# Norm sums taken on VectorE, and the query projection folded into 512-column matmuls

## The chip, the cores and the metric

The kernel runs on one core of a Trainium2 chip. The core has five engines that each work through a queue of their own in order: TensorE (PE, matmuls; its weight loads are listed as PEld), VectorE (DVE), ScalarE (ACT), GpSimd (POOL) and SyncE (SP, which here only issues transfers). The metric is device microseconds of one execution; the time of a kernel is the median of its runs. A profile is one more execution with the hardware profiler on.

## The reference

Two decoder layers on 256 tokens of 2048 features, batch 1, all in float32. Layer 0 mixes a causal gMLP (8 heads) with an HGRN2 recurrence (8 heads of 128 features); layer 1 mixes by forgetting attention (16 heads). Each mixer is followed by a gated MLP with a width-3 causal convolution. Cut to what the change touches:

```python
def rms_norm(x, gain):
    y = x * lax.rsqrt(jnp.mean(x * x, axis=-1, keepdims=True) + RMS_EPS)
    return y * gain

def mixer_ab(h, w_in, ...):          # layer 0, h = rms_norm(x)
    u, v, q, f, i, g = jnp.split(h @ w_in, cuts, axis=-1)
    ...
    y_b = hgrn2(q, f, i, g, lower_bound, o_gain)
    return jnp.concatenate([y_a, y_b], axis=-1) @ w_out

for l in range(2):
    h = rms_norm(x, mix_norm[l]);  x = x + mixer(h)
    h = rms_norm(x, ffn_norm[l]);  x = x + conv_ffn(h)
```

So there are four norms over the 2048 features of each token, and one projection of 2048 x 1024 for the queries `q` of the recurrence.

## The kernel before

**Tiles.** Activations lie feature-major: a tile has 128 features in its partitions and 256 tokens as columns. Every float32 operand of a large product is split into a high part and a low part (fp32r), and a product is high times high, high times low, and low times high, summed in PSUM. An activation tile `a` has 512 columns: the 256 high ones, then the 256 low ones. A weight tile `w` arrives by a transfer on SP's queue; ScalarE copies its high part `wh` (L185), VectorE subtracts for its low part `wl` (L186). This goes on for all 820 weight pieces, and TensorE consumes them in order.

**Norms.** The gain is multiplied into the activations when they are split, and the factor `Rt`, one number per token, is applied later, when a product leaves PSUM. `Norm.feed_square` adds the squares of the 16 feature tiles into `acc` (128 x 256). `Norm.finish_tok` (L466) has TensorE sum `acc` over its partitions: two small matmuls, `acc` as the stationary operand and a two-column piece of ones as the moving one (L470), which the profile counts as four. `rsq` (L425 to L430, with Ln and Exp on ScalarE between) makes `Rt` of the sums. It runs four times: at the start of layer 0, before each gated MLP, and before layer 1.

**Queries.** In `mixer_ab` the queries are projected head by head (L876), `project` with the weights stationary: per 128 features, the high weights times the 256 high columns, the high weights times the 256 low columns, and the low weights times the 256 high columns, all into the same 256 columns of a PSUM bank (L316). ScalarE then copies the even and the odd tokens into the head's tile `kq` (L877, L878), the odd ones in reverse. `project` also makes the last four blocks of the last product of the kernel; the change leaves these as they are.

**Around them.** A recurrence head is a generator `hgrn(h)` whose steps are laid between the weight pieces of the projections that come next: per head a copy to `kd` on ScalarE (L741), two products on GpSimd (L742 on `kd`, L744 on `kq`), a chain of six products on GpSimd (L750, `tot`), small diagonal matmuls on TensorE (L755), and products and copies on VectorE and ScalarE (L762 to L805). Between the heads 3 and 4, and 6 and 7, `values(j)` projects the recurrence's values (`project_tok`): there TensorE reads a mirrored copy `ar` of the activations, which GpSimd makes piece by piece (L332), in a rotation of three buffers.

**The order.** The program is written as one stream; a scheduling layer then sets each engine's queue, under the explicit "not before" ties (`held`, `tied`, `in_order`). An engine never runs past a waiting instruction.

Of the kernel before, what the change touches and what calls it, by code (L numbers as in the profile page):

```python
# [8 lines left out]
F32 = mybir.dt.float32  # L9
F32R = mybir.dt.float32r  # L10
U16 = mybir.dt.uint16
AF = mybir.ActivationFunctionType
ALU = mybir.AluOpType
AX = mybir.AxisListType

P = 128
S = 256
D = 2048
# [6 lines left out]
BLK = 32  # L25
# [9 lines left out]
LANE = 64  # L35
# [20 lines left out]
def tile_trunk(ctx: ExitStack, tc: tile.TileContext, x, pp_d, cst_d, mlev_d, msk_d,  # L56
               w_v, w_f, w_g, w_i, w_q, w_u, w_abo, w_cf, w_cqkv, w_cg, w_co, w_up, w_dn, spw_d, spb_d, out):
    nc = tc.nc
    V, SC, PE = nc.vector, nc.scalar, nc.tensor

    cp = ctx.enter_context(tc.tile_pool(name="cp", bufs=1))
    wp = ctx.enter_context(tc.tile_pool(name="wp", bufs=4))
    apool = ctx.enter_context(tc.tile_pool(name="ap", bufs=KT))
    tp = ctx.enter_context(tc.tile_pool(name="tp", bufs=2))
# [4 lines left out]
    def nm(base):  # L69
        count[0] += 1  # L70
        return f"{base}_{count[0]}"
# [3 lines left out]
    for c0, n in ((0, 1), (1, 1), (2, 2), (4, 2), (6, 2), (8, 4), (12, 4)):  # L75
        t = cp.tile([P, n, S], F32, tag=f"x{c0}", name=f"x{c0}")
# [4 lines left out]
    ones = cp.tile([P, P], F32, tag="ones", name="ones")  # L81
# [5 lines left out]
    order = mybir.DependencyInfo(mybir.DependencyClass.NoSync, mybir.DependencyReason.DATA)  # L87
    epoch = {"set": None, "load": None, "ops": []}

    def act(out_, in_, func, **kw):  # L90
        name = TABLE.get(func)
        if name is not None and name != epoch["set"]:
            ld = SC.preload_act_table_set(name)
            for o in epoch["ops"]:
                tc.add_manual_dep(ld.ins, o.ins.name, order, reason="table order")
            epoch.update(set=name, load=ld, ops=[ld])
        r = SC.activation(out_, in_, func, **kw)
        if name is not None:
            tc.add_manual_dep(r.ins, epoch["load"].ins.name, order, reason="table order")
            epoch["ops"].append(r)  # L100
        return r

    def view(ap, off, *dims):
        return bass.AP(ap.tensor, ap.offset + off, [list(ap.ap[0])] + [list(d) for d in dims])

    def back(ap):
        return view(ap, P - 1, (-1, P))
# [5 lines left out]
    def bank():  # L113
        return psum["pool"].tile([P, 512], F32, tag="px", name=nm("px"), bufs=psum["banks"])
# [11 lines left out]
    def tick():  # L126
        steps[0] += 1
        while queue and len(flight) < depth[0]:
            flight.append(queue.pop(0))
        for g in list(flight):  # L130
            if next(g, flight) is flight:
                flight.remove(g)
# [16 lines left out]
    deep = {"pool": None, "turn": 0, "dma": None}  # L149
# [39 lines left out]
    before = {}  # L189
# [6 lines left out]
    def weights(src, n, rows=None, parts=halves):  # L196
        w, wh, wl = three(n)
        in_order("w", nc.sync.dma_start(w if rows is None else w.rearrange("p (m c) -> p m c", m=rows), src))
        parts(w, wh, wl)
        for what in ("wh", "wl"):  # L200
            in_order(what, deep[what])
        return wh, wl
# [89 lines left out]
    def by_tokens(t, o):  # L292
        return view(t, o, (1, P), (P, 2))

    def to_tokens(ps):
        return view(ps, 0, (2, P), (1, 2))

    def of_tokens(ps, T):
        return view(ps, T, (2, P))

    def project(wsrc, acts, chunks=(8, 8), k0=0, run=2, parts=None):

        ps = pm.tile([P, 512], F32, tag="pm", name=nm("pm"))
        nk = sum(chunks)
        done = 0
        for c in chunks:
            lo = (k0 + done) * P
            if parts is None:
                tick()
            wh, wl = parts or weights(wsrc[:, lo:lo + c * P], c * P)  # L310
            for k1 in range(0, c, run):
                ks = range(k1, min(k1 + run, c))
                for t, os in ((wh, (0, S)), (wl, (0,))):
                    for k in ks:
                        for o in os:
                            deep["last"] = PE.matmul(to_tokens(ps), t[:, k * P:(k + 1) * P],  # L316
                                                     by_tokens(acts[done + k], o),
                                                     start=done + k + o == 0 and t is wh,
                                                     stop=t is wl and done + k == nk - 1)
            done += c  # L320
        return ps
# [82 lines left out]
    def held(r, last="wh"):  # L404

        tc.add_manual_dep(r.ins, deep[last].ins.name, order, reason="not before")
# [13 lines left out]
    def rsq(dst, src, n):  # L420
        tag = "sq" if dst.shape[-1] == S else "rm"
        cols = dst.shape[-1] if dst.shape[-1] == S else LANE // math.prod(dst.shape[1:-1])
        m, t = (tp.tile(list(dst.shape[:-1]) + [max(cols, dst.shape[-1])], F32, tag=tag, name=nm(n_))
                [..., 0:dst.shape[-1]] for n_ in ("rm", "rt"))
        V.tensor_scalar(m, src, 1.0 / n, EPS, ALU.mult, ALU.add)  # L425
        act(dst, m, AF.Ln)
        act(dst, dst, AF.Exp, scale=-0.5)
        V.scalar_tensor_tensor(t, dst, -0.5, dst, ALU.mult, ALU.mult)
        V.tensor_tensor(t, t, m, ALU.mult)
        V.scalar_tensor_tensor(dst, t, 1.5, dst, ALU.add, ALU.mult)  # L430
# [5 lines left out]
    class Norm:  # L436
# [27 lines left out]
            self.feed_square(k)  # L464

        def finish_tok(self):  # L466
            p2 = bank()
            for T in range(2):
                lhs = self.acc[:, T * P:(T + 1) * P] if not self.turn else view(self.acc, T, (2, P))
                r = PE.matmul(p2[:, 2 * T:2 * T + 2], lhs, ones[:, 0:2], start=True, stop=True)  # L470
                if "mm" in deep:
                    tc.add_manual_dep(r.ins, deep["mm"].ins.name, order, reason="not before")
            Rt = cp.tile([P, LANE], F32, tag="Rt", name=nm("Rt"), bufs=2)[:, 0:2]
            yield
            yield
            rsq(Rt, p2[:, 0:4].rearrange("p (t two) -> p t two", two=2)[:, :, 0], D)
            self.Rt = Rt

    def add_four(q, ps, z, tmp, dst, nxt, halves=1, queues=(nc.sync, nc.gpsimd)):
# [25 lines left out]
    def mixer_ab(norm):  # L505
        es = ExitStack()
        hp = es.enter_context(tc.tile_pool(name="hp", bufs=1))
# [23 lines left out]
        for g, ps in enumerate(project_first(w_v, norm, lambda: queue.append(finish()))):  # L531
# [5 lines left out]
            else:  # L537
                last = ps
        A = norm.a
# [19 lines left out]
        two = hp.tile([P, 2, P], F32, tag="pairs", name="pairs")  # L559
# [109 lines left out]
        lf, kq = [], []  # L669
# [20 lines left out]
        for j in range(2):  # L690
            ps = project_four(w_f[4 * j:4 * j + 4], A, KT)
            Rt = norm.Rt
            z, tmp = (hp.tile([P, 1024], F32, tag="E", name=nm(n), bufs=2) for n in ("zf", "tmp"))
            for T in range(2):
                SC.activation(cols4(z[:, T * 512:(T + 1) * 512]), of_rows(ps[T]), AF.Copy, scale=Rt[:, T:T + 1])
            t = hp.tile([P, 1024], F32, tag="o", name=nm("turn"), bufs=2)
# [137 lines left out]
        def values(j):  # L834
            ps = project_tok(w_i[j], norm, lambda: hp.tile([P, 512], F32R, tag="ar", name=nm("ar"), bufs=3))
            itok = hp.tile([P, 2, 512], F32, tag="tok", name=nm("itok"), bufs=2)
            for T in range(2):
                SC.activation(cols2(itok[:, T]), of_two(ps[T]), AF.Copy, scale=Rr[:, T:T + 1])
            itoks.append((itok, steps[0]))
# [29 lines left out]
        for h in range(NH):  # L869
            if h in (4, 7):  # L870
                values(len(itoks))
            while len(kq) <= h:
                tick()
            if h % 4 == 0:
                os_.append(hp.tile([P, 2, 512], F32, tag="o", name=nm("o"), bufs=2))
            ps = project(w_q[h], A)  # L876
            SC.activation(kq[h][:, 2], of_tokens(ps, 0), AF.Copy)  # L877
            SC.activation(back(kq[h][:, 1]), of_tokens(ps, 1), AF.Copy)  # L878
            queue.append(hgrn(h))
        for j in range(2):  # L880
            ps = project_four(w_g[4 * j:4 * j + 4], A, KT)
# [16 lines left out]
        for j in range(2):  # L898
            ps = project_four(w_u[4 * j:4 * j + 4], A, KT)
            z, tmp = (hp.tile([P, 1024], F32, tag="E", name=nm(n), bufs=2) for n in ("zu", "tmp"))  # L900
            for T in range(2):
                SC.activation(cols4(z[:, T * 512:(T + 1) * 512]), of_rows(ps[T]), AF.Copy, scale=Rt[:, T:T + 1])
            t = hp.tile([P, 1024], F32, tag="tok", name=nm("turn"), bufs=2)
# [12 lines left out]
        def stretch(q, ks, **kw):  # L916
            return project_four(w_abo[4 * q:4 * q + 4], product, KT, ks=ks, **kw)

        ahead = None
        for q in range(4):  # L920
            if q == 0:

                ps = stretch(0, (0, 2, 4, 6, 8, 10), more=True)
                ahead = stretch(1, (0, 2, 4, 6), more=True)
                stretch(0, (12, 14), ps=ps)
            elif q == 1:
                ps = stretch(1, (8, 10, 12, 14), ps=ahead)
            else:
                ps = stretch(q, range(0, KT, 2))
            z = hp.tile([P, 2, 512], F32, tag="tok", name=nm("zo"), bufs=2)  # L930
# [323 lines left out]
    def ffn(l, norm, last):  # L1254
# [142 lines left out]
        return nxt  # L1397

    norm = mixer_ab(Norm(C_MIX))
    norm = ffn(0, norm, False)  # L1400
    norm = mixer_c(norm)
# [81 lines left out]
```

## Time and profile before

| what | us |
|---|---|
| median of 3 runs | 2170.12 (2169.95 to 2170.48) |
| the profiled execution | 2170.68 |
| its span on the core | 2168.9 |
| TensorE matmuls busy | 2162.4 |
| VectorE busy | 1599.7 |
| ScalarE busy | 1310.1 |
| GpSimd busy | 470.7 |

The granted TensorE clock is 1.00 over the span. Times in the profile's views count from the span's start. A matmul's duration in a view holds its way through the pipeline; the pace at which matmuls follow each other is read from their starts. "Idle before" is the time in which an engine stood still ahead of an instruction, with what ended it.

### The profile page before, as it was taken

The numbers are of one execution on the slowest core, as the hardware profiler recorded it, in microseconds if no ns is written. First come the engines' busy times: TensorE is split into PE (matmuls) and PEld (weight loads), VectorE is DVE, ScalarE is ACT, GpSimd is POOL, SyncE is SP. The second block draws the span as 40 slices with busy tenths as digits, with TensorE's granted clock in tenths as the row PEclk, the third lists the DMA queues.
The fourth block names the chain that finished last, engine by engine and source line by source line (L and its number), as shares of the span: only waits on it lengthen the run. The fifth ranks groups of instructions, "written<-read, shape, count | busy, mean of one in ns | idle before, by whom it ended". The sixth has DMA issues, their size and how long they took to land.

```text
span 2168.9 us, 32423 instructions
## 1 busy us (share of the span) xinstructions
PE 2162.4 (100%) x10874; PEld 1900.3 (88%) x10874; DVE 1599.7 (74%) x2265; ACT 1310.1 (60%) x1903; POOL 470.7 (22%) x867
## 2 busy tenths in 40 slices
PE   9999999999999999999999999999999999999999
PEld 8998888888888888888888888888888888888888
DVE  7888768777577657776887787877786577667766
ACT  6677766666466545654565556766666466456642
POOL 0352231212012002111133443221211012012102
PEclk9999999999999999999999999999999999999999
DMA  8755777777667767776777767777777677666866
GB/s 304 220 172 175 219 223 236 235 229 238 217 214 223 223 213 212 230 235 205 248 230 223 243 203 215 225 240 223 234 238 223 201 236 220 227 213 208 247 214 187
DMA packets 492680, 483.61 MB, mean 223 GB/s; under 512 B 115168, under 2 KB 460400, under 8 KB 492384
## 3 DMA queue, kind: packets, MB, share of 16 engines
q1 hardware_dynamic: 465888, 453.27, 66.4%
q0 software_dynamic: 24896, 26.05, 5.2%
q10 hardware_dynamic: 1728, 2.21, 0.4%
q8 instruction: 85, 1.39, 0.3%
q14 instruction: 83, 0.68, 0.1%
HBM read 435.24 MB, written 2.11 MB: 202 GB/s over the span
## 4 chain that ended last, share of the span: by engine, by line
PE 94%; DVE 2%; DMA 2%; SPq 1%; ACT 1%; issue 0%; DVEq 0%; ACTq 0%; POOLq 0%
PE pm L360 25%; PE pm L361 25%; PE pm L362 25%; PE pm L341 4%; PE pm L343 4%; PE pm L342 4%; PE pm L316 2%; PE pm L236 1%; DVE wl L186 1%; SPq L380 1%; DMA w<-in_w_up 1%; DMA zt<-tmp 1%; PE pm L260 0%; DVE tmp L373 0%; ACT wh L185 0%
## 5 line engine op out<-in xcount | busy, mean ns | idle before, releaser
L186 DVE TENSOR_TENSOR wl<-w,wh 128x1024 fp32r<-128x1024 f32 (+1 forms) x820 | 991.6, 1217 | 460.6 <-ACT wh L185 451.1
L185 ACT ACTIVATE wh<-w 128x1024 fp32r<-128x1024 f32 (+1 forms) x820 | 856.7, 1049 | 624.4 <-PE pm L362 459.3
L360 PE MATMUL pm<-wh,a 128*128 128x512 f32 x1728 | 655.8, 379 | 0.0
L361 PE MATMUL pm<-wl,a 128*128 128x512 f32 x1728 | 655.2, 379 | 0.2
L362 PE MATMUL pm<-wh,a 128*128 128x512 f32 x1728 | 654.9, 379 | 0.0
L380 POOL DMA_DIRECT2D zt<-tmp x413 | 223.5, 549 | 1134.8 <-DVE tmp L373 1022.9
L361 PEld LDWEIGHTS pm<-wl,a 128*128 128x128 f32 x1728 | 326.6, 189 | 47.1 <-DVE wl L186 1.0
L362 PEld LDWEIGHTS pm<-wh,a 128*128 128x128 f32 x1728 | 326.6, 189 | 46.3
L360 PEld LDWEIGHTS pm<-wh,a 128*128 128x128 f32 x1728 | 326.6, 189 | 46.3
L360 PE MATMUL pm<-wh,hid 128*128 128x512 f32 x688 | 260.8, 379 | 0.0
L361 PE MATMUL pm<-wl,hid 128*128 128x512 f32 x688 | 260.8, 379 | 0.0
L362 PE MATMUL pm<-wh,hid 128*128 128x512 f32 x688 | 260.8, 379 | 0.0
L341 PE MATMUL pm<-wh,a 128*128 128x512 f32 x416 | 158.7, 381 | 0.4 <-ACT a L398 0.4
L343 PE MATMUL pm<-wh,a 128*128 128x512 f32 x416 | 157.8, 379 | 0.0
L342 PE MATMUL pm<-wl,a 128*128 128x512 f32 x416 | 157.7, 379 | 0.0
L360 PEld LDWEIGHTS pm<-wh,hid 128*128 128x128 f32 x688 | 130.0, 189 | 18.5
L362 PEld LDWEIGHTS pm<-wh,hid 128*128 128x128 f32 x688 | 130.0, 189 | 18.4
L361 PEld LDWEIGHTS pm<-wl,hid 128*128 128x128 f32 x688 | 130.0, 189 | 18.4
L1289 ACT ACTIVATE conv<-zt,pp 128x256 f32<-128x256 f32 x176 | 95.8, 589 | 71.5 <-DMA zt<-tmp 48.4
L380 POOL DMA_DIRECT2D turn<-tmp x160 | 86.9, 551 | 211.4 <-DVE tmp L373 179.3
L1290 DVE SCALAR_TENSOR_TENSOR conv<-zt,pp,conv 128x255 f32<-128x255 f32 x176 | 80.2, 480 | 54.4 <-ACT conv L1289 42.7
L373 DVE STREAM_TRANSPOSE tmp<-z 128x512 f32<-128x512 f32 x120 | 98.1, 850 | 7.1 <-ACT z L1275 5.1
(255 smaller groups left out, 2207.7 us busy)
## 6 DMA issues: line engine op xcount, KB each, us to landing
w<-in_w_up SPq DMA_DIRECT2D x352, 512.0 KB, 5.0
w<-in_w_dn SPq DMA_DIRECT2D x176, 512.0 KB, 5.0
w<-in_w_cqkv SPq DMA_DIRECT2D x96, 512.0 KB, 4.9
w<-in_w_abo SPq DMA_DIRECT2D x32, 512.0 KB, 5.0
w<-in_w_cg SPq DMA_DIRECT2D x32, 512.0 KB, 5.2
w<-in_w_co SPq DMA_DIRECT2D x32, 512.0 KB, 4.8
zt<-tmp SPq DMA_DIRECT2D x414, 32.0 KB, 2.7
zt<-tmp POOLq DMA_DIRECT2D x413, 32.0 KB, 2.4
```

Source lines behind the costliest of these rows:

```text
L185: r = deep["wh"] = SC.activation(wh, w, AF.Copy)
L186: deep["wl"] = V.tensor_tensor(wl, w, wh.bitcast(F32), ALU.subtract)
L341: PE.matmul(to_two(ps[T]), ah, h, start=k + i == 0, stop=False)
L342: PE.matmul(to_two(ps[T]), ah, l, start=False, stop=False)
L343: deep["last"] = PE.matmul(to_two(ps[T]), al, h, start=False, stop=k + i == KT - 1)
L360: PE.matmul(to_rows(ps[T]), ah, h, start=not begun and k + i == ks[0], stop=False)
L361: PE.matmul(to_rows(ps[T]), ah, l, start=False, stop=False)
L362: deep["mm"] = deep["last"] = PE.matmul(to_rows(ps[T]), al, h, start=False, stop=not more and k + i == ks[-1] + 1)
L373: V.transpose(tmp.rearrange("p (b m i t) -> p b m i t", b=4, m=4, t=2)[:, :, :, :, T], src(T).rearrange("p (m b j) -> p b m j", m=4, b=4))
L380: queues[(a + b) % len(queues)].dma_start(dst[BLK * b:BLK * (b + 1), :, a * n:(a + 1) * n], tmp[BLK * a:BLK * (a + 1), b * 4 * n:(b + 1) * ...
L1289: held(SC.activation(c, z, AF.Identity, bias=pp[:, cb:cb + 1], scale=w(2)))
L1290: V.scalar_tensor_tensor(c[:, 1:], z[:, :S - 1], w(1), c[:, 1:], ALU.mult, ALU.add)
```

## The change

Two edits. First, `finish_tok` no longer uses TensorE: VectorE transposes `acc` in blocks of 32 x 32, sums each block's columns, brings the four partition quarters side by side with four small copies, sums these, and copies the result out to the four quarters; `rsq` then reads that instead of PSUM. Second, the query projection gets `fold=True`: the high weights meet the high and the low columns of the activations in one 512-column matmul, high result in columns 0 to 255 and low result in 256 to 511; the low weights still go in a 256-column matmul onto the first half. One ScalarE copy takes all 512 columns to SBUF (a tile `z` in the same three-buffer rotation as `ar`), and GpSimd adds the halves, once for the even and once for the odd tokens.

```diff
     def project(wsrc, acts, chunks=(8, 8), k0=0, run=2, parts=None, fold=False):
...
+                if fold:
+                    for k in ks:
+                        PE.matmul(ps, wh[:, k * P:(k + 1) * P], view(acts[done + k], 0, (S, 2), (1, P), (P, 2)),
+                                  start=done + k == 0, stop=False, skip_group_check=True)
+                    for k in ks:
+                        deep["last"] = PE.matmul(to_tokens(ps), wl[:, k * P:(k + 1) * P],
+                                                 by_tokens(acts[done + k], 0),
+                                                 start=False, stop=done + k == nk - 1, skip_group_check=True)
+                    continue
...
         def finish_tok(self):
-            p2 = bank()
-            for T in range(2):
-                lhs = self.acc[:, T * P:(T + 1) * P] if not self.turn else view(self.acc, T, (2, P))
-                r = PE.matmul(p2[:, 2 * T:2 * T + 2], lhs, ones[:, 0:2], start=True, stop=True)
-                if "mm" in deep:
-                    tc.add_manual_dep(r.ins, deep["mm"].ins.name, order, reason="not before")
-            Rt = cp.tile([P, LANE], F32, tag="Rt", name=nm("Rt"), bufs=2)[:, 0:2]
+            t = cp.tile([P, LANE], F32, tag="Rt", name=nm("Rt"), bufs=2)
+            Rt, ssq, r, u, s = (t[:, i:i + n] for i, n in ((0, 2), (2, 2), (8, 8), (16, 32), (48, 8)))
+            sq = tp.tile([P, S], F32, tag="sq", name=nm("sq"))
+            by_block = view(self.acc, 0, (1, 2), (2 * BLK, 4), (2, BLK)) if self.turn else \
+                self.acc.rearrange("p (t g i) -> p t g i", t=2, i=BLK)
+            held(V.transpose(sq.rearrange("p (t g i) -> p t g i", t=2, i=BLK), by_block), "wl")
+            held(V.tensor_reduce(r, sq.rearrange("p (c i) -> p c i", i=BLK), AX.X, ALU.add), "wl")
             yield
+            for a in range(4):
+                held(V.tensor_copy(u[0:BLK, 8 * a:8 * a + 8], r[BLK * a:BLK * (a + 1)]), "wl")
+            V.tensor_reduce(s[0:BLK], u[0:BLK].rearrange("p (a c) -> p c a", a=4), AX.X, ALU.add)
+            for g in range(4):
+                V.tensor_copy(ssq[BLK * g:BLK * (g + 1)], view(s[0:BLK], g, (4, 2)))
             yield
-            rsq(Rt, p2[:, 0:4].rearrange("p (t two) -> p t two", two=2)[:, :, 0], D)
+            rsq(Rt, ssq, D)
...
-            ps = project(w_q[h], A)
-            SC.activation(kq[h][:, 2], of_tokens(ps, 0), AF.Copy)
-            SC.activation(back(kq[h][:, 1]), of_tokens(ps, 1), AF.Copy)
+            ps = project(w_q[h], A, fold=True)
+            z = hp.tile([P, 512], F32, tag="ar", name=nm("z"), bufs=3)
+            SC.activation(z, ps, AF.Copy)
+            for i, q in enumerate((kq[h][:, 2], back(kq[h][:, 1]))):
+                nc.gpsimd.tensor_tensor(q, view(z, i, (2, P)), view(z, S + i, (2, P)), ALU.add)
```

TensorE's queue keeps its order, without the four pairs of small matmuls. Three places of other queues move.

GpSimd, around the start of `values(1)`, after head 6's projection; `ar_1965`, `ar_2003`, `ar_2071` are the first three mirrored pieces of `values(1)`, and `kd_1584` and `kq_1007` belong to head 3. Before:

```order
L742 TENSOR_TENSOR kd_1584<-kd_1584,kq_1007 128x2x64
L744 TENSOR_TENSOR kq_1007<-kq_1007,lf_1006 128x2x64
L332 COPY ar_1965<-a_113 128x256
L332 COPY ar_1965<-a_120 128x256
L332 COPY ar_2003<-a_162 128x256
L332 COPY ar_2003<-a_169 128x256
L332 COPY ar_2071<-a_207 128x256
L332 COPY ar_2071<-a_210 128x256
L750 TENSOR_TENSOR tot_1790<-lf_1223 128x128
```

The same three mirrored pieces now (`ar_1876`, `ar_1914`, `ar_1982`); `kd_1896` and `kq_1224` are head 5's, and L894 is the pair of adds of head 6:

```order
L756 TENSOR_TENSOR kd_1896<-kd_1896,kq_1224 128x2x64
L758 TENSOR_TENSOR kq_1224<-kq_1224,lf_1223 128x2x64
L341 COPY ar_1876<-a_113 128x256
L341 COPY ar_1876<-a_120 128x256
L341 COPY ar_1914<-a_162 128x256
L894 TENSOR_TENSOR kq_1276<-z_1853 128x128 x2
L341 COPY ar_1914<-a_169 128x256
L341 COPY ar_1982<-a_207 128x256
L341 COPY ar_1982<-a_210 128x256
```

The pieces stood behind head 3's products, far ahead of their use; now they stand behind head 5's, and head 6's adds stand among them. At `values(0)` they move in the same way, from ahead of head 0's products to behind head 1's.

VectorE, at the first norm; `acc_90` is its sum of squares, `wl_...` are weight pieces of the projection that runs then, `rm_596` and `rm_605` are the first step of `rsq`. Before:

```order
L186 TENSOR_TENSOR wl_535<-w_533,wh_534 128x1024
L564 CAST msk<-kst 128x896
L659 TENSOR_TENSOR gm<-gm 128x8
L660 TENSOR_TENSOR gm<-gm 128x8
L186 TENSOR_TENSOR wl_561<-w_559,wh_560 128x1024
L569 TENSOR_TENSOR wt_511<-wt_511,cst 128x1024
L661 RECIPROCAL gm<-gm 128x8
L662 TENSOR_TENSOR gm<-gm 128x8
L663 TENSOR_TENSOR gm<-gm 128x8
L186 TENSOR_TENSOR wl_580<-w_578,wh_579 128x1024
L664 TENSOR_SCALAR gm<-gm 128x8
L425 TENSOR_SCALAR rm_596<-px_551 128x2
```

Now:

```order
L186 TENSOR_TENSOR wl_535<-w_533,wh_534 128x1024
L481 STREAM_TRANSPOSE sq_552<-acc_90 128x256
L578 CAST msk<-kst 128x896
L482 TENSOR_REDUCE Rt_551<-sq_552 128x8
L186 TENSOR_TENSOR wl_561<-w_559,wh_560 128x1024
L485 COPY Rt_551<-Rt_551 32x8 x4
L583 TENSOR_TENSOR wt_511<-wt_511,cst 128x1024
L486 TENSOR_REDUCE Rt_551<-Rt_551 32x8
L186 TENSOR_TENSOR wl_589<-w_587,wh_588 128x1024
L488 COPY Rt_551<-Rt_551 32x2 x4
L673 TENSOR_TENSOR gm<-gm 128x8
L434 TENSOR_SCALAR rm_605<-Rt_551 128x2
```

Eleven new instructions stand between the weight pieces, and `rm` stays behind the same third piece. At the other three norms the eleven stand together after one piece or around one, and `rm` comes up to two pieces earlier than before.

ScalarE, after head 7's projection; `z_2266` is the new copy, `kd` the copy of L741 (now L755), `wh_2479` and `wh_2376` the same weight piece. Before:

```order
L93 ACT_TABLE_LOAD
L877 ACTIVATE kq_1361<-pm_2283 128x128
L878 ACTIVATE kq_1361<-pm_2283 128x128
L769 ACTIVATE E_2253<-kq_1323 128x256
L741 ACTIVATE kd_2431<-kq_1361 128x2x64
L794 ACTIVATE s_366_2401<-px_2375 128x128
L796 ACTIVATE st_953<-px_2375 64x64 x2
L185 ACTIVATE wh_2479<-w_2478 128x1024
```

Now:

```order
L93 ACT_TABLE_LOAD
L892 ACTIVATE z_2266<-pm_2194 128x512
L783 ACTIVATE E_2164<-kq_1276 128x256
L808 ACTIVATE s_374_2298<-px_2272 128x128
L810 ACTIVATE st_962<-px_2272 64x64 x2
L755 ACTIVATE kd_2328<-kq_1314 128x2x64
L185 ACTIVATE wh_2376<-w_2375 128x1024
```

The copy to `kd` has moved behind three others, directly ahead of the weight piece. It reads the head's tile `kq`, which GpSimd's adds now write: where it waited for ScalarE's own copies, it now waits for GpSimd.

More of the change, by code (lines that the diff above doesn't have):

```diff
@@ L299, in of_tokens, with project @@
         return view(ps, T, (2, P))
-    def project(wsrc, acts, chunks=(8, 8), k0=0, run=2, parts=None):
+    def project(wsrc, acts, chunks=(8, 8), k0=0, run=2, parts=None, fold=False):
         ps = pm.tile([P, 512], F32, tag="pm", name=nm("pm"))
```

## The prediction

> **What bounds the kernel now.** I read the page's first part (busy time, share of the span and instructions of each engine), and then its fourth, the chain of work that ended last.
>
> ```profile
> PE 2162.4 (100%) x10874; PEld 1900.3 (88%) x10874; DVE 1599.7 (74%) x2265; ACT 1310.1 (60%) x1903; POOL 470.7 (22%) x867
> PE 94%; DVE 2%; DMA 2%; SPq 1%; ACT 1%; issue 0%; DVEq 0%; ACTq 0%; POOLq 0%
> ```
>
> TensorE is busy for 2162.4 of 2168.9 us and makes 94% of the chain. So work taken off TensorE shortens the span one for one, as long as TensorE then waits for nothing new; time on other engines counts only where TensorE comes to wait for it. Two questions follow: what TensorE's queue loses, and where its next operand now comes too late.
>
> **What leaves TensorE: the norms.** TensorE's timeline at the first and at the last of the four norms (start, duration, instruction):
>
> ```profile
> 49.51 0.38 PE L362 MATMUL pm<-wh,a 128*128 128x512 f32 x1
> 49.72 0.50 PE L470 MATMUL px<-ones,acc 128*128 128x2 f32 x4
> 50.09 0.46 PE L360 MATMUL pm<-wh,a 128*128 128x512 f32 x1
> 50.39 0.38 PE L361 MATMUL pm<-wl,a 128*128 128x512 f32 x1
> ...
> 1505.27 0.38 PE L362 MATMUL pm<-wh,a 128*128 128x512 f32 x1
> ...
> 1506.16 0.38 PE L361 MATMUL pm<-wl,a 128*128 128x512 f32 x1
> ```
>
> From L362's start to that of the second matmul behind it (L361) are 0.88 and 0.89 us. Two 512-column steps take 2 x 0.216 (next fence), so one norm costs 0.45 us of TensorE, and four cost **1.8 us**.
>
> **The queries.** Two pieces of the chain, and the group of high-weight matmuls of L316:
>
> ```profile
> 16.22 31.08 PE pm L236 x144
> 181.21 5.36 PE pm L316 x48
> L316 PE MATMUL pm<-a,wh 128*128 128x256 f32 x256 | 39.7, 278 | 0.0
> ```
>
> 144 matmuls of 512 columns take 31.08 us, 215.8 ns each; 48 of 256 columns take 5.36 us, 111.7 ns each. Two small ones cost 223.4, so each pair that becomes one saves 7.5 ns. The 256 matmuls of the group are 128 pairs: **1.0 us**. The low-weight matmuls stay. The Trainium skill ("TensorE: Matmul & The Clock Gate", Part 1, "Wait — 56ns, not 53.3ns?") gives a warm step as columns over 2.4 GHz and about 2.5 ns more; this agrees with the 215.8, but makes 109.2 ns of the 256 columns, where the trace has 111.7. By the page the 128 pairs would save 0.3 us; the measured rows decide.
>
> Together TensorE's queue gets 2.8 us shorter. All else of this part is what comes back as waits.
>
> **Norms on VectorE.** Groups of VectorE that are most like the new instructions (busy us, mean ns):
>
> ```profile
> L373 DVE STREAM_TRANSPOSE tmp<-z 128x512 f32<-128x512 f32 x120 | 98.1, 850 | 7.1 <-ACT z L1275 5.1 <-ACT z L481 1.5
> L1082 DVE TENSOR_REDUCE mxs<-sc 128x1 f32<-128x256 f32 x16 | 6.5, 409 | 0.0
> L643 DVE COPY small<-rab 32x1 f32<-32x1 f32 x4 | 0.6, 145 | 0.1
> ```
>
> The transpose has half the columns of L373's (0.43), the big reduction is like L1082 (0.41), eight copies at L643's 0.145 make 1.16, the small reduction I put at 0.2, since it has an eighth of that one's columns but can't be shorter than a small copy: some 2.2 us of VectorE per norm. The timeline of ScalarE, VectorE and TensorE behind the first norm, and one row of VectorE at the second:
>
> ```profile
> 54.64 1.05 ACT L185 ACTIVATE wh<-w 128x1024 fp32r<-128x1024 f32 x1
> 55.72 1.22 DVE L186 TENSOR_TENSOR wl<-w,wh 128x1024 fp32r<-128x1024 f32 x1 [0.49 <-ACT wh L185]
> 58.16 0.38 PE L361 MATMUL pm<-wl,a 128*128 128x512 f32 x1
> ...
> 383.40 2.36 DVE L186 TENSOR_TENSOR wl<-w,wh 128x1024 fp32r<-128x1024 f32 x2 [1.36 <-ACT wh L185]
> ```
>
> In the last three norms VectorE stands idle 1.36 us ahead of each weight piece, so two pieces take it in; I cost them at 0 (bounds 0 and 0.3). Their `Rt` then comes a piece or two earlier, and with it SP issues one transfer of `turn` two weight pieces sooner; I cost that at 0 too, since weights there are split a whole piece ahead (the second wl of the row at 383.40 belongs to the piece after next).
>
> The first norm has less room: VectorE's queue is full there, and behind `rsq` stands ScalarE's table load, then `gv`, then wh at 54.64 and its wl, which ends at 56.94, 1.22 us ahead of its matmul at 58.16. Part of the eleven fits where VectorE waited for other things; I take wh to come 0.85 later, still hidden, and charge 0.1 us. If all 2.2 us arrived there, it would be 1.0.
>
> **The adds on GpSimd.** A ScalarE copy with the new one's form, and the products on GpSimd that are most like the adds (minimum, median, maximum in ns):
>
> ```profile
> L838 ACT ACTIVATE itok<-pm,small 128x512 f32<-128x512 f32 x4 | 2.6, 681 | 0.1
> L742 POOL TENSOR_TENSOR kd<-kd,kq x8: 517/902/1486, 97.1 to 190.4; 128x128 f32<-128x128 f32 x8
> L744 POOL TENSOR_TENSOR kq<-kq,lf x8: 507/576/851, 98.1 to 191.2; 128x128 f32<-128x128 f32 x8
> ```
>
> ScalarE gives up two copies of 0.26 (L877 in the next fence, and its sister) and gets one of 0.68. A pair of adds is bounded by the fastest and the slowest product: 1.0 and 3.0 us. I take twice L744's median, **1.15 us**, since its operands, as the adds', are float32 128 x 128 read with a stride; twice L742's median would be 1.8. None of it is on TensorE, so it counts where TensorE soon needs what stands behind the adds. There are four such places; rows of `values(0)`, head 4 and `values(1)`:
>
> ```profile
> 116.28 0.26 ACT L877 ACTIVATE kq<-pm 128x128 f32<-128x128 f32 x1
> 119.48 0.38 PE L341 MATMUL pm<-wh,ar 128*128 128x512 f32 x1
> 148.40 0.52 POOL L744 TENSOR_TENSOR kq<-kq,lf 128x128 f32<-128x128 f32 x1
> 150.22 0.33 PE L755 MATMUL px<-kq,kd 128*32 128x32 f32 x16
> L332 POOL CAST ar<-a 128x256 fp32r<-128x256 f32 x32 | 20.9, 690 | 1.5 <-PE pm L343 1.5
> 156.66 0.39 ACT L741 ACTIVATE kd<-kq 128x128 f32<-128x128 f32 x1
> 155.30 0.98 DVE L740 RECIPROCAL kd<-lf 128x128 f32<-128x128 f32 x1
> 157.13 1.27 POOL L742 TENSOR_TENSOR kd<-kd,kq 128x128 f32<-128x128 f32 x1 [0.96 <-ACT kd L741]
> 158.48 0.57 POOL L744 TENSOR_TENSOR kq<-kq,lf 128x128 f32<-128x128 f32 x1
> 157.91 0.38 PE L341 MATMUL pm<-wh,ar 128*128 128x512 f32 x1
> ```
>
> - `values(0)`: head 3's copy starts in ScalarE's slot at 116.28 and ends near 116.96; the adds end at 118.1, the second half of the second mirrored piece (L332, 0.69) at 118.8; TensorE needs it at 119.48. Charged 0.2, bounds 0 and 1.0.
> - Head 4: `kq` is ready at 148.92, needed at 150.22; adds ahead of it take 0.6 of that 1.3. Charged 0, bounds 0 and 0.5.
> - `values(1)`, the dearest: its first mirrored half now stands behind head 5's products. Before, these ended at 159.05; TensorE wants the half at 157.91. In ScalarE's queue the weight piece that stood ahead of `kd`'s copy now stands one place earlier, so the copy can go when VectorE's reciprocal is done (156.28, from 155.30 and 0.98) instead of at 156.66, some 0.35 sooner. The products (0.9 and 0.57, from 156.8) end near 158.4, the half (0.69) at 159.1: **1.2 us** of wait. Bounds: 0.5 with the fastest product and a mirror copy of 0.4, 1.9 with the old start and 1.27. It is inside a stretch where TensorE had no wait at all, so all of it shows.
> - Head 7, as the projection of the gates starts, on its own rows:
>
> ```profile
> 190.79 2.02 ACT L185 ACTIVATE wh<-w 128x1024 fp32r<-128x1024 f32 x2
> 191.22 0.85 POOL L744 TENSOR_TENSOR kq<-kq,lf 128x128 f32<-128x128 f32 x1
> 192.38 1.26 DVE L186 TENSOR_TENSOR wl<-w,wh 128x1024 fp32r<-128x1024 f32 x1
> 193.40 0.33 PE L755 MATMUL px<-kq,kd 128*32 128x32 f32 x16
> 193.98 0.38 PE L361 MATMUL pm<-wl,a 128*128 128x512 f32 x1
> ```
>
> ScalarE's copy to `kd` now waits for GpSimd's adds, and behind it on ScalarE waits the weight piece of 190.79. The adds can end near 191.15, so wh starts about 0.7 late, its wl about 0.2 late of a lead of 0.34 (193.98 less 193.64), and `kq`, ready at 192.07 before, comes at 193.3 for 193.40. Charged 0.3, bounds 0 and 1.8.
>
> **The sum.** 0.1 + 0.2 + 0 + 1.2 + 0.3 = 1.8 us comes back of 2.8; net 1.0. The profiled execution took 2170.68, 0.56 above the median of the runs, so it would become 2169.7 and the median **2169.1 us**. All upper bounds at once (1.0 + 0.3 + 1.0 + 0.5 + 1.9 + 1.8 = 6.5) would give 2173.8, all lower ones (0.5) 2167.8.
>
> **The rivals.**
>
> *GpSimd's adds are slow.* One mechanism, with its price per place: beyond the margins above, every us by which a pair is longer than 1.15 delays the mirrored half behind head 6's adds in `values(1)` and the `kd` copy of head 7 fully, `values(0)` and head 4 only beyond a further 0.6 and 0.7. At 1.8 a pair, this adds 0.65 + 0.6 + 0.1 = 1.35 us: 2170.5, slower than before. At 3.0 it adds 1.85 + 1.75 + 1.2 + 1.1 = 5.9: 2175. It decides from a pair of about 1.7 on, where 2 x 0.55 eats the net 1.0. For it speaks that L742 varies by three, and that its 1.27 at 157.13 lay beside VectorE's work; against it, that the L744s, always next in GpSimd's queue, stay near 0.58. The Trainium skill ("SBUF — State Buffer", "Who interferes with whom") says that VectorE and GpSimd share a port pair under an exclusive lock, which speaks against moving adds there; the spread of L742 fits it, though no row shows a lock.
>
> *All is hidden.* If head 5's products run at their fastest and the mirror copy starts when its operands are there, `values(1)` costs 0.5 or less and the rest nothing: 2170.1 - 2.8 + 0.3 = 2167.6. For it speaks that TensorE's 2162.4 busy us leave only 6.5 for all its waits before, so the order has so far kept such places clear; against it, that a queue can't pass its head, and head 5's products stand there.
>
> *The fold saves nothing.* The 111.7 ns is read from a run of mixed high and low matmuls. If the low-weight matmul behind a 512-column one is slower by what the pair saves, only the norms' 1.8 is left: 2170.1.
>
> **How the numbers follow.** Forecast 0.53; slow adds 0.22; all hidden 0.17; no saving from the fold 0.05; others 0.03. The predicted time is 2169.1. The forecast's own spread is 2168.3 to 2170.3; the range goes down to the hidden case with a little more (2167.2) and up into the slow adds past their median price (2172.5). A measurement of this kernel tells about 0.2%, 4.3 us, from no change: below 2165.8 or above 2174.5. Faster by that much would need more than TensorE gives up: 0.02. Slower needs the slow adds near their maximum, or something not seen: 0.05. Within: 0.93.
>
> **What would show it.** In the changed profile TensorE's 16 small matmuls of L470 are gone, and between L362 and the next L361 at each norm lie two plain steps. The queries show steps of 215.8 and 111.7 ns alternating by pairs. Right for `values(1)`: TensorE's first matmul on a mirrored piece there shows idle time of 0.5 to 1.9 us ended by GpSimd; wrong, if there is none. Right for head 7: the copy to `kd` on ScalarE waits for GpSimd, and TensorE shows at most some tenths behind it. A pair of adds should last 1.0 to 1.4 us; from 1.7 on the first rival holds. Wrong as a whole would be a wait at the first norm over 1 us, or one at a place not named here.

## The result, and the profile after

| | before | after |
|---|---|---|
| median of 10 runs, us | 2170.20 (2169.02 to 2172.40) | 2175.45 (2174.31 to 2176.66) |
| ratio, 95% interval | | 1.0024 [1.0016, 1.0032] |
| profiled execution, us (span) | 2170.68 (2168.9) | 2176.24 (2174.5) |

The change makes the kernel 5.25 us slower. That is outside the predicted range (2167.2 to 2172.5). Ratios and intervals, here and below, leave out three executions that lasted much longer than the others of their kernel: one of `norm_only` (5130 us) and two of the kernel before (2839 and 5940 us). The first part of the page after, and its chain:

```profile
PE 2164.0 (100%) x10730; PEld 1896.8 (87%) x10730; DVE 1608.7 (74%) x2309; ACT 1314.0 (60%) x1895; POOL 480.9 (22%) x883
PE 93%; DVE 2%; DMA 1%; ACT 1%; SPq 1%; issue 1%; POOL 1%; DVEq 0%; ACTq 0%; POOLq 0%
```

GpSimd has come into the chain with 1%. TensorE has 144 matmuls fewer and yet 1.6 us more busy time, which can't be if its steps were as long as before. The view of TensorE's waits (whom it waited for, us in total, times, longest) of after, and the largest row of before behind its start:

```profile
PE pm L350 <- POOL ar L341: 3.5, 1, 3.5
PE pm L350 <- ACT a L407: 1.0, 1, 1.0
PE pm L370 <- DVE wl L186: 0.5, 1, 0.5
...
PE pm L341 <- ACT a L398: 0.4, 1, 0.4
```

The second row, 1.0 us for an activation tile at 1064.22, is the wait of 0.4 before grown by 0.6; it stands ahead of the third norm, and what lengthened it was not followed. One new wait stands out: 3.5 us for a mirrored piece (L341 is `project_tok`'s copy, L332 before). TensorE's timeline there, at the start of `values(1)`:

```profile
158.32 0.38 PE L352 MATMUL pm<-wh,a 128*128 128x512 f32 x1
162.16 0.80 PE L350 MATMUL pm<-wh,ar 128*128 128x512 f32 x1 [3.46 <-POOL ar L341]
162.75 0.63 PE L351 MATMUL pm<-wl,ar 128*128 128x512 f32 x1
163.18 0.63 PE L352 MATMUL pm<-wh,ar 128*128 128x512 f32 x1
...
167.44 0.49 PE L350 MATMUL pm<-wh,ar 128*128 128x512 f32 x1
167.77 0.38 PE L351 MATMUL pm<-wl,ar 128*128 128x512 f32 x1
```

From 158.32 to 162.16 are 3.84 us where a step is 0.216: a wait of **3.62 us**. Behind it the steps are 0.43 us long, until 167.77. 13 steps take 5.61 us instead of 2.81: another **2.80 us** are lost without any wait. Why, the granted clock tells (view by windows; the third number from the end is PEclk):

```profile
150.00:158.00 8.00, 8.00 (x111) 7.33 (x110) 6.45 (x14) 5.83 (x12) 3.61 (x9) 1.00 0.59 176
162.00:165.00 3.00, 2.84 (x7) 2.30 (x8) 0.81 (x2) 0.55 (x3) 3.00 (x8) 0.50 0.71 234
168.00:175.00 7.00, 7.00 (x94) 6.12 (x93) 5.01 (x13) 4.45 (x11) 3.44 (x11) 1.00 0.50 151
```

The clock was full, then half, then full again: the trace has it at half for 6.8 us, from 160.84 on, so the last 1.3 us of the wait are among them. Over the span it is 0.998 instead of 1.000, which is easily overlooked. The Trainium skill ("TensorE: Matmul & The Clock Gate", "HAM oscillation — how this bites in real kernels") warns of idle gaps of TensorE over about 3.4 us for this. The wait here is longer, 3.62 us, but the clock fell 2.3 us into it, since the next step was due at 158.54.

Why the piece was late shows in ScalarE's, GpSimd's and VectorE's timelines:

```profile
154.03 0.58 ACT L892 ACTIVATE z<-pm 128x512 f32<-128x512 f32 x1
154.68 1.56 POOL L894 TENSOR_TENSOR kq<-z 128x128 f32<-128x128 f32 x2 [4.00 <-ACT z L892]
157.10 0.94 DVE L754 RECIPROCAL kd<-lf 128x128 f32<-128x128 f32 x1
158.13 0.42 ACT L755 ACTIVATE kd<-kq 128x128 f32<-128x128 f32 x1 [0.56 <-DVE kd L754]
156.21 0.49 POOL L764 TENSOR_TENSOR tot<-lf 128x128 f32<-128x128 f32 x1
156.77 1.86 POOL L764 TENSOR_TENSOR tot<-tot 128x64 f32<-128x64 f32 x5
158.62 1.49 POOL L756 TENSOR_TENSOR kd<-kd,kq 128x128 f32<-128x128 f32 x1
160.19 0.57 POOL L758 TENSOR_TENSOR kq<-kq,lf 128x128 f32<-128x128 f32 x1
160.72 1.39 POOL L341 CAST ar<-a 128x256 fp32r<-128x256 f32 x1
158.54 1.20 DVE L186 TENSOR_TENSOR wl<-w,wh 128x1024 fp32r<-128x1024 f32 x1
160.32 1.53 DVE L186 TENSOR_TENSOR wl<-w,wh 128x1024 fp32r<-128x1024 f32 x1
```

GpSimd works without a gap from head 5's adds on: adds, the six `tot` products, the two products, the mirrored half. Two of these are stretched to more than twice their best time (0.52 for L756 at head 4, 0.40 for the copy), and both lie beside a VectorE subtraction. The products could hardly have started sooner, though: they also need `kd`, and ScalarE's copy of it, which waits for VectorE's reciprocal, ends at 158.55. So two chains end together there, `tot` behind the adds on GpSimd (158.63) and the reciprocal with the copy on the other two engines. The second is late as well: the reciprocal ends at 158.04, 1.76 later than before (156.28), where TensorE comes only 0.63 later (157.16 for 156.53 at the start of `values(1)`).

Most of the rest lies at the first norm. Two rows of VectorE and one of ScalarE before, then rows of VectorE, ScalarE and TensorE after:

```profile
46.35 0.63 DVE L564 CAST msk<-kst 128x896 uint16<-128x896 f32 x1 [1.88 <-DMA kst<-in_msk]
52.12 0.15 DVE L425 TENSOR_SCALAR rm<-px 128x2 f32<-128x2 f32 x1
54.06 0.69 ACT L97 ACTIVATE gv<-pm,Rt 128x512 f32<-128x512 f32 x1
...
47.32 0.63 DVE L578 CAST msk<-kst 128x896 uint16<-128x896 f32 x1 [2.01 <-DMA kst<-in_msk]
49.32 1.41 DVE L485 COPY Rt<-Rt 32x8 f32<-32x8 f32 x4
53.94 0.16 DVE L434 TENSOR_SCALAR rm<-Rt 128x2 f32<-128x2 f32 x1
56.57 0.69 ACT L97 ACTIVATE gv<-pm,Rt 128x512 f32<-128x512 f32 x1 [0.70 <-DVE Rt L439]
58.60 0.38 PE L369 MATMUL pm<-wh,a 128*128 128x512 f32 x1
59.52 0.48 PE L370 MATMUL pm<-wl,a 128*128 128x512 f32 x1 [0.53 <-DVE wl L186]
59.84 0.38 PE L371 MATMUL pm<-wh,a 128*128 128x512 f32 x1
```

`rm` comes at 53.94 instead of 52.12. So the wl of the piece behind it is late: 58.60 to 59.84 are 1.24 us for two steps of 0.43, 0.81 lost. Two smaller delays of the same kind at 52.8 and 55.8 cost 0.36 and 0.26. In all **1.4 us**.

The account: -1.8 (four norms) - 1.0 (the fold) + 1.4 + 3.6 + 2.8 = +5.0. The two profiled executions, from which these terms are read, lie 5.6 us apart, the medians 5.25. Of the 0.6 that is missing, 0.5 is there before anything of the change has run: the matmuls of L236 start at 16.54, before at 16.05 (in the other kernels below between 15.55 and 16.44). The 0.6 at 1064.22 is nearly made up by 0.4 that only the profile before loses, at 880.37. The fold's saving is there: two 512-column and two 256-column steps of the queries now take 0.655 us, where six of 111.7 ns took 0.670; 64 such groups make 1.0 us.

### The profile page after: what moved, and what is told of

Its sections match the earlier page's. It is cut to its first block, busy times and chain, and to the rows that moved or that the text cites. A ratio compares the mean times of both kernels' runs of the same rounds, so it can differ in the third digit from the quotient of the medians.

```text
span 2174.5 us, 32193 instructions
## 1 busy us (share of the span) xinstructions
PE 2164.0 (100%) x10730; PEld 1896.8 (87%) x10730; DVE 1608.7 (74%) x2309; ACT 1314.0 (60%) x1895; POOL 480.9 (22%) x883
## 3 DMA queue, kind: packets, MB, share of 16 engines
q8 instruction: 84, 1.38, 0.3%
## 4 chain that ended last, share of the span: by engine, by line
PE 93%; DVE 2%; DMA 1%; ACT 1%; SPq 1%; issue 1%; POOL 1%; DVEq 0%; ACTq 0%; POOLq 0%
PE pm L370 25%; PE pm L369 25%; PE pm L371 25%; PE pm L350 4%; PE pm L352 4%; PE pm L351 4%; PE pm L315 1%; PE pm L236 1%; SPq L389 1%; DVE wl L186 1%; PE pm L260 1%; PE pm L318 1%; ACT wh L185 1%; DVE tmp L382 0%; DMA zt<-tmp 0%
```

## Experiments

Each ratio is against runs of the kernel before on the same chip. Besides times, the granted clock over the span is given for each kernel's runs, since half a clock shows there: the 6.8 us of the change's profiled run as 0.998, the 3.4 us in that of `fold_only` as 0.999. Three of the ten runs of the change have 0.998 and seven 0.999, so most of its runs seem to have lost less to the clock than the profiled one.

### Each part alone

`fold_only` undoes the norm part, `norm_only` the query part:

```diff
 fold_only:  finish_tok as before the change (TensorE)
 norm_only:
-            ps = project(w_q[h], A, fold=True)
...
+            ps = project(w_q[h], A)
+            SC.activation(kq[h][:, 2], of_tokens(ps, 0), AF.Copy)
+            SC.activation(back(kq[h][:, 1]), of_tokens(ps, 1), AF.Copy)
```

> The queries as in the changed kernel, the four norms on TensorE as before. Theory: the whole loss is in values(1), where TensorE waited 3.6 us for the first mirrored piece and then ran 5.3 us at half its clock (2.8 us more); the fold saves 1.0 on TensorE. So 2170.2 - 1.0 + 6.4 = 2175.6 us, with a wait of 3 to 4 us on the first mirrored piece of values(1) and steps of 427 ns behind it. Rival, the norms on VectorE carry the loss: below 2170.

> The norms' sums on VectorE, the queries as before. Theory: four norms save 1.8 us of TensorE, and the first norm gives 1.4 back in three waits for weights between 52 and 60 us: 2170.2 - 1.8 + 1.4 = 2169.8 us, no wait in values(1). Rival, the norms carry the loss: above 2174.

`fold_only`: 2175.11 us against 2169.92, ratio 1.0025 [1.0015, 1.0034]. `norm_only`: 2170.74 without the one long execution, ratio 1.0005 [0.9996, 1.0015], so no difference that can be told; 0.82 above the kernel before where -0.4 was expected, with the first norm's delays in its trace; the interval holds both. TensorE's waits in `fold_only`:

```profile
PE pm L350 <- POOL ar L341: 4.5, 2, 3.1
```

The loss belongs to the queries, as expected. There are two waits for mirrored pieces here: one in `values(1)`, and one of 1.4 in `values(0)`, which the whole change doesn't have.

### The mirrored pieces put ahead again

In `own_z` the halves go into two tiles of 256 columns from another pool; the rotation holds mirrored pieces only, and GpSimd's order has the first three pieces of `values(1)` behind head 3's products, as before the change.

```diff
-            z = hp.tile([P, 512], F32, tag="ar", name=nm("z"), bufs=3)
-            SC.activation(z, ps, AF.Copy)
+            hi, lo = (tp.tile([P, S], F32, tag="sq", name=nm(n)) for n in ("zh", "zl"))
+            SC.activation(hi, ps[:, 0:S], AF.Copy)
+            SC.activation(lo, ps[:, S:2 * S], AF.Copy)
...
-                nc.gpsimd.tensor_tensor(q, view(z, i, (2, P)), view(z, S + i, (2, P)), ALU.add)
+                nc.gpsimd.tensor_tensor(q, view(hi, i, (2, P)), view(lo, i, (2, P)), ALU.add)
```

> The changed kernel, but the two halves of the query projection go into tiles of their own (two ScalarE copies of 256 columns) and not into the rotation of the mirrored pieces, so the first three mirrored pieces of values(1) stand far ahead on GpSimd again. Theory: the wait of 3.6 us and the half clock behind it go, 2175.45 - 6.4 = 2169.1 us, with the same adds on GpSimd. Rival, the adds themselves (or their contention with VectorE) cost the time: 2174 or more.

2173.84 us (2171.30 to 2174.79), ratio 1.0017 [1.0008, 1.0026]: neither number. The wait in `values(1)` is gone, but another has come, at head 7, which TensorE's and GpSimd's timelines show:

```profile
195.42 0.33 PE L769 MATMUL px<-kq,kd 128*32 128x32 f32 x16 [2.08 <-POOL kq L758]
191.16 1.70 POOL L895 TENSOR_TENSOR kq<-zh,zl 128x128 f32<-128x128 f32 x2 [0.45 <-ACT zl L893]
193.30 1.48 POOL L756 TENSOR_TENSOR kd<-kd,kq 128x128 f32<-128x128 f32 x1 [0.44 <-ACT kd L755]
194.86 0.51 POOL L758 TENSOR_TENSOR kq<-kq,lf 128x128 f32<-128x128 f32 x1
```

This is the prediction's fourth place. In the changed kernel TensorE doesn't wait there: it is 7 us later at this point than in `own_z`, while GpSimd's work for head 7 is only 4.8 us later (its `tot` starts at 192.16, and at 187.39 in `own_z`). The first wait hid the second. The runs also fall into two groups: four have a clock of 1.000 (2171.30 to 2173.65 us), six 0.999 (2173.72 to 2174.79). So the wait here, 2.1 us in the profiled run, the fastest of the ten, halves the clock in some runs and not in others; how long it is in those is not known.

### Is it ScalarE's copy to kd?

The copy to `kd` of head 4 waits 0.54 us for the adds on ScalarE. `kd_pool` gives it to GpSimd.

```diff
-            SC.activation(view(kd, 0, (P + 1, 2), (2, H)), view(t, 0, (3 * P + 1, 2), (2, H)), AF.Copy)
+            nc.gpsimd.tensor_copy(view(kd, 0, (P + 1, 2), (2, H)), view(t, 0, (3 * P + 1, 2), (2, H)))
```

> The changed kernel, but GpSimd makes the copy to kd in place of ScalarE, so ScalarE no longer stands behind GpSimd's adds at head 4. Theory: the chain of head 3 and with it head 5's products come about 1 us sooner, TensorE's wait in values(1) shrinks from 3.6 to about 2.6 us, too short to take the clock down, so that 1.0 + 2.8 us go: 2171.6 us. Rival, the wait at head 4 has no part in it: the wait in values(1) stays at 3.6 or grows by GpSimd's copy, the half clock stays, 2175.5 to 2176.

2174.99 us, ratio 1.0023 [1.0013, 1.0032]. The theory fell: the wait stayed. TensorE and GpSimd:

```profile
162.29 0.80 PE L350 MATMUL pm<-wh,ar 128*128 128x512 f32 x1 [3.42 <-POOL ar L341]
154.35 1.55 POOL L894 TENSOR_TENSOR kq<-z 128x128 f32<-128x128 f32 x2 [3.38 <-ACT z L892]
156.43 1.92 POOL L764 TENSOR_TENSOR tot<-tot 128x64 f32<-128x64 f32 x5
158.29 1.30 POOL L755 COPY kd<-kq 128x128 f32<-128x128 f32 x1
```

The adds of head 5 start and `tot` ends some 0.3 sooner than in the changed kernel, no more, and GpSimd's own copy takes that up. In this kernel GpSimd's queue sets the time: adds, `tot`, copy, products, piece, one behind the other, from head 5's copy on. The run takes the copy out of one of the changed kernel's two chains, but puts it into the other.

### How long a wait takes the clock down

`delay8` and `delay10` are the kernel before, with the fourth mirrored piece of `values(1)` written eight or ten times over:

```diff
-                for i in range(2):
+                for i in [0, 1] * (8 if k == 6 and steps[0] > deep["d0"] else 1):
                     nc.gpsimd.tensor_copy(ar[:, i * S:(i + 1) * S].rearrange("p (u n) -> p u n", u=2),
...
+            deep["d0"] = 10 ** 9 if h < 7 else 0
```

> The kernel before, but GpSimd writes the fourth mirrored piece of values(1) eight times over, so that TensorE waits for it. Theory on the clock: a wait of TensorE of about 2 us or more can take its clock to half for some us behind it, and whether it does differs from run to run, as in own_z (granted clock 0.999 in the slow ones of its runs, 1.000 in the fast ones). With some 2 us of wait expected here: 2172 us where the clock stays, 2174 to 2175 where it goes. Rival, only the wait itself counts: all runs within 1 us of 2172.

> The same with ten times. Theory: a wait of some 4 us, and the clock goes to half behind it in every run, for 3 to 5 us: 2169.9 + 4 + 2 to 3 = 2176 to 2177 us. Rival: 2174.

`delay8` 2171.79 us, ratio 1.0008 [0.9999, 1.0017]; `delay10` 2175.93, ratio 1.0027 [1.0016, 1.0037]. TensorE's timeline in `delay8` (two rows), then in `delay10`:

```profile
168.11 0.48 PE L341 MATMUL pm<-wh,ar 128*128 128x512 f32 x1 [1.06 <-POOL ar L332]
168.43 0.38 PE L342 MATMUL pm<-wl,ar 128*128 128x512 f32 x1
...
169.79 0.48 PE L341 MATMUL pm<-wh,ar 128*128 128x512 f32 x1 [2.88 <-POOL ar L332]
...
171.12 0.79 PE L341 MATMUL pm<-wh,ar 128*128 128x512 f32 x1 [0.42 <-POOL ar L332]
171.71 0.63 PE L342 MATMUL pm<-wl,ar 128*128 128x512 f32 x1
```

The wait came out at 1.2 us in `delay8`, shorter than the 2 us meant, and the time rose by 1.9; so this run doesn't test a wait of 2 us. In `delay10` there are 3.0 and 0.6 us, and then steps of half clock; a third wait in its trace, 1.9 us for a weight at 1593.12, left the clock full. With the other kernels, the wait in the profiled run and the clocks of all runs give a scale. The waits are reckoned from the starts, as the 3.62 above, which gives 0.1 to 0.2 more than the views' idle times:

| kernel | wait, us | runs with a clock under 1.000 |
|---|---|---|
| delay8 | 1.2 | 0 of 10 |
| own_z | 2.1 (in its fastest run, clock 1.000) | 6 of 10 |
| fold_dve, fold_dve_late (below) | 2.7 | 4 of 10, 6 of 10 |
| delay10 | 3.0, then 0.6 | 8 of 8 |
| fold_only | 3.2 | 10 of 10 |
| kd_pool | 3.6 | 7 of 9 |
| after | 3.6 | 10 of 10 |

The clock is at half for 3.4 us in the traces of `fold_only`, `kd_pool`, `delay10` and `fold_dve_late`, and for 6.8 in that of the change. What that costs shows between runs of one kernel: those with 0.999 lie 1.5 us above those with 1.000 in `own_z`, 1.7 in `fold_dve` and 1.1 in `fold_dve_late` (medians).

### The adds off GpSimd

In `fold_dve` ScalarE copies the low half only, and VectorE adds it to the high half out of PSUM; norms as before. `fold_dve_late` takes the last three norms to VectorE and leaves the first on TensorE.

```diff
+            lo = tp.tile([P, S], F32, tag="sq", name=nm("zl"))
+            SC.activation(lo, ps[:, S:2 * S], AF.Copy)
...
+                V.tensor_tensor(q, view(ps, i, (2, P)), view(lo, i, (2, P)), ALU.add)
```

> The queries folded as in the changed kernel, but only the low half is copied by ScalarE (256 columns, not in the mirrored pieces' rotation) and VectorE adds it to the high half out of PSUM; the four norms on TensorE as before. Theory: the loss came with the adds' place in GpSimd's queue, not with the fold; without them the fold's 1.0 us shows, 2169.9 - 1.0 = 2168.9 us, with no wait of TensorE on GpSimd. Rival, the fold or its longer ScalarE copy itself delays the recurrence: 2171 or more.

> As fold_dve, and the last three norms' sums by VectorE, the first norm's by TensorE. Theory: only the first norm on VectorE costs waits (1.4 us of its 0.45), the three others save 3 x 0.45: 2169.9 - 1.0 - 1.4 = 2167.5 us, faster than before by 2.4. Rival, the norms' work on VectorE is paid elsewhere too: 2169 or more.

2172.90 us, ratio 1.0014 [1.0004, 1.0023], and 2172.78, ratio 1.0014 [1.0004, 1.0023]. Both expectations fail, though there is no add on GpSimd now. TensorE's waits in `fold_dve` name the place:

```profile
PE px L764 <- POOL kq L753: 2.7, 1, 2.7
```

It is head 7 again, whose second add now stands in VectorE's queue behind two products of 512 columns:

```profile
190.71 1.28 DVE L838 TENSOR_TENSOR o<-o,small 128x512 f32<-128x512 f32 x2
191.91 0.28 DVE L889 TENSOR_TENSOR kq<-pm,zl 128x128 f32<-128x128 f32 x1
```

So the rival (the fold delays the recurrence) holds at head 7, whichever engine adds.

### Without head 7

Three kernels project head 7's queries as before and fold the others: `own_z7` (adds on GpSimd, all norms on VectorE), `own_z7_late` (the first norm on TensorE), `fold_dve7_late` (adds on VectorE, first norm on TensorE).

```diff
+            if h < NH - 1:
                 ps = project(w_q[h], A, fold=True)
...
+            else:
+                ps = project(w_q[h], A)
+                SC.activation(kq[h][:, 2], of_tokens(ps, 0), AF.Copy)
+                SC.activation(back(kq[h][:, 1]), of_tokens(ps, 1), AF.Copy)
```

> As own_z (adds on GpSimd, halves in tiles of their own, all norms on VectorE), but head 7's queries are projected as before, without fold and adds. Theory: the fold has two places where what stands behind the adds is late, the mirrored pieces of values(1) and head 7's products at the start of the gates; with both gone the adds of heads 0 to 6 cost TensorE nothing and the clock stays: 2169.9 - 0.84 (7 heads) - 1.8 + 1.4 (first norm) = 2168.7 us, granted clock 1.000 in all runs. Rival, the adds on GpSimd cost time by contention wherever they stand: 2171 or more.

> As own_z7, with the first norm's sums by TensorE. Theory: the first norm on VectorE costs 1.4 and saves 0.45, so this is 0.95 us faster than own_z7: 2167.7 us. Rival, VectorE takes the first norm without loss as well: 0.45 slower than own_z7, 2169.2.

> As fold_dve_late (VectorE adds the halves, first norm by TensorE, three by VectorE), but head 7's queries as before. Theory: head 7 was the only place with a loss there (a wait of 2.7 us on GpSimd's product and, in half of the runs, the half clock): 2169.9 - 0.84 - 1.36 = 2167.7 us. Rival, what was lost at head 7 comes up at the next place: 2170 or more.

2170.61 us, ratio 1.0003 [0.9994, 1.0013]; 2170.23, ratio 0.9997 [0.9988, 1.0007]; 2169.14, ratio 0.9997 [0.9987, 1.0007]. The clock is 1.000 in all 30 runs. All three are level with the kernel before, and all are faster than the change. None reaches its expectation; the waits left in `own_z7` are small and many:

```profile
PE pm L370 <- DVE wl L186: 1.3, 3, 0.5
PE pm L351 <- DVE wl L186: 0.5, 1, 0.5
```

They are for weights on VectorE, at the first norm, in `values(1)`, behind head 7 and at 1587.19, far behind the queries. `fold_dve7_late` has the lowest median of all kernels tried, 1.1 us under that of the kernel before, which its interval doesn't tell from none.

## Why the prediction was wrong

- **What bounds the kernel, and the 2.8 us that TensorE gives up:** right. The norms' matmuls are gone and the fold saves its 1.0, though not by steps of 215.8 and 111.7 as worked out: a group has 218, 216, 109 and 112 ns.
- **The norms:** no wait of TensorE is seen at the last three, as said. The first was charged 0.1 and cost 1.4 us. The step taken was that wh comes 0.85 later and is still hidden. `rm` came 1.8 later, but of this 0.97 was there at the mask's cast ahead of it; from the cast's start to `rm` it is 6.62 where it was 5.77, so the norm's own share, 0.85, came out as charged, in part by luck, since the four copies of the quarters took 1.41 us there in place of the 0.58 assumed. Two things were left out. Five small instructions on `gm`, which stood ahead of `rm` before, now stand behind it, and from `rm` to `gv` it is 2.63 where it was 1.94: 0.7 more. And TensorE itself comes 0.45 sooner, its own matmuls being gone. 0.85 + 0.7 + 0.45 = 2.0 is more than the lead of 1.22. In `own_z`, where the cast comes as early as before, the first norm costs 0.9; in the four other traces with it on VectorE 1.3 to 1.5.
- **`values(1)`:** the place, the engine and the mechanism were right, and the size was wrong, by two steps. The working let the copy to `kd` go when the reciprocal is done, at 156.28, and head 5's products start "from 156.8", which is 157.4 in the changed kernel's time; they started at 158.6, 1.2 late. It had priced head 6's adds, but not head 5's, which stand ahead of `tot`, which stands ahead of the products; and it had the reciprocal at its old time, where it came 1.8 later. It had charged head 4 with 0, since TensorE doesn't wait there; but ScalarE does (0.54 us, for the adds), and its later work came late too, head 5's copy `z` among it (154.03, where the copies to `kq` began at 152.27), and behind that both the adds and the reciprocal. Each of the two chains, as measured, reaches to within 0.1 of the products' start. The second step: it took 0.9 for the product and 0.69 for the mirrored half; they took 1.49 and 1.39, which makes up the other 1.2. 1.2 forecast, 3.6 measured; `own_z` shows that the wait goes with the order.
- **What a wait costs:** the sum charged every us of wait as one us. Behind this one the clock was halved, 2.8 us more in the profiled run. The prediction named no such case; its bound of 1.9 for the wait lay under the 3.4 us of the Trainium skill. This and the late products are why the time left the range.
- **`values(0)` and head 4:** no wait in the changed kernel. Without the first norm's delay `values(0)` has one of 1.4 to 1.6 (`fold_only`), so the bound of 1.0 was too small as well.
- **Head 7:** charged 0.3, and nothing in the changed kernel, but only because TensorE was late already: 2.1 us in `own_z`, 2.7 in `fold_dve`, above the bound of 1.8 as it stood. The wait is for `kq`, which the prediction had ready 0.1 ahead of its use.
- **The rivals:** a pair of adds took 1.4 us at the median (16 adds of 509 to 1071 ns, median 697), within the 1.0 to 1.4 expected and under the 1.7 from which slow adds were to decide. That rival had the sign, but not the mechanism: the adds count by where they stand. That its time for pairs of 3.0 us, 2175, comes near the measured one is luck. "All is hidden" fails; the fold does save.

Not settled is why the three kernels without head 7 stay 1.4 to 2.5 us above their expectations (0.3 of it is the kernel before, 2170.2 on that chip and 2169.9 in the expectations). The small waits for VectorE's weights are seen, but no run takes them away one by one.

## What to carry to other kernels

On an engine that works its queue in order, list everything that is queued between the released instruction and the one that the bounding engine needs, with the previous step's new work too, and add up the whole run; head 5's adds take 1.56 us themselves, and 6.4 were lost behind them. Follow each operand of that instruction back as well: here two chains were late by the same time, and moving work from one to the other gained nothing that can be told. If the bounding engine is TensorE, price a wait over 2 us with the half clock behind it, as one case with its own time. A buffer rotation shared by two uses ties their orders together: give the new tile a buffer of its own before putting it there. And when a wait is removed, look for the next one that its delay had covered.

## What the runs showed of the hardware

- The clock went to half in about half of the runs of the kernels whose traces show a wait of TensorE of 2.1 to 2.7 us, and in 35 of 37 runs of those with 3.0 to 3.6 (table above), for 3.4 us in four traces and 6.8 in one. In the trace of the change it fell 2.3 us into the wait. At 2.7 us one trace has the full clock (`fold_dve`) and one the half (`fold_dve_late`). So it can come below the 3.4 us of idle that the Trainium skill names in the section cited above, and it depends on the run. In `fold_dve_late` the half begins only 1.3 us after the wait has ended (at 196.68, the wait ends at 195.37).
- GpSimd was held up beside VectorE's subtractions. With VectorE idle, mirrored copies take 0.40; the one started at 160.72, beside the subtraction from 160.32 to 161.85, ended 0.26 behind it (162.11). L756, started at 158.62 beside a subtraction to 159.74, ended 0.37 behind it. The Trainium skill ("SBUF — State Buffer", "Who interferes with whom") states an exclusive lock for a whole instruction of the other engine; these two rows agree with it. It goes the other way too: two of the four quarter copies of the first norm, 0.42 and 0.63 us where the others take 0.16, end at 49.74 and 50.56, 0.02 and 0.03 behind GpSimd's instructions of 48.34 (1.38 us) and 49.80 (0.73 us).
- In the folded queries a 256-column step took 109 ns ahead of another one, and 112 ahead of a 512-column one.
